# A hybrid mLSTM and stick-breaking layer: gate rows in 128-byte runs, one block transposition, other copy buffers, and a later place for a sigmoid

## The chip, the cores and the metric

The kernel runs on one NeuronCore of one Trainium2 chip. A NeuronCore has five engines that run side by side, each with a queue of its own that is worked off in order: TensorE (PE in the profile, with its weight loads as PEld), VectorE (DVE), ScalarE (ACT), GpSimd (POOL) and SyncE (SP). SyncE computes nothing; here it issues most of the DMAs. An engine that waits for a semaphore holds up everything that stands behind the waiting instruction in its queue. The metric is the device time of one execution in microseconds; lower is better.

## The reference, cut to what matters

One layer on x of shape (1, 512, 1024), float32. A normalised input is projected to all columns at once; two token mixers (an mLSTM with 4 heads of 256, a stick-breaking attention with 8 heads of 128) work on parts of the projection, and their outputs are gated, merged and projected back.

```python
h = rmsnorm(x, norm_w)
proj = jnp.einsum('bsd,de->bse', h, w_in) + b_in
(mq, mk, mv, mi, mf, mo, mz, sq, sk, sv, sz, gates) = jnp.split(proj, split_at, axis=-1)

qk = jax.nn.silu(causal_depthwise_conv(jnp.concatenate([mq, mk], axis=-1), conv_w, conv_b))
mq_c, mk_c = jnp.split(qk, 2, axis=-1)
log_i = mi.astype(jnp.float32).transpose(0, 2, 1)                     # (1, 4, 512)
log_f = jax.nn.log_sigmoid(mf.astype(jnp.float32)).transpose(0, 2, 1) # (1, 4, 512)
hm = mlstm_chunkwise(to_heads(mq_c, M_HEADS), to_heads(mk_c, M_HEADS),
                     to_heads(mv, M_HEADS), log_i, log_f)
hm = rmsnorm(hm..., mlstm_norm_w...)
y_m = hm * jax.nn.sigmoid(mo) * jax.nn.silu(mz)

qs = rmsnorm(to_heads(sq, SB_HEADS), sb_q_norm_w)
ks_ = rmsnorm(to_heads(sk, SB_HEADS), sb_k_norm_w)
y_s = stick_breaking_attention(qs, ks_, to_heads(sv, SB_HEADS)) * jax.nn.silu(sz)

merged = g_m * (y_m @ w_proj_m) + g_s * (y_s @ w_proj_s)   # g = sigmoid(gates)
x = x + merged @ w_out
```

Inside `mlstm_chunkwise` the two gate rows of each head are turned into running sums of log_f and a running maximum; weights are exp(b_t - b_s + i_s - m_t), and the denominator is at least exp(-m_t).

## The kernel before, in words

**Units and steps.** The matrix work is cut into 136 units, listed in `units`. A unit is one block of weights: it is loaded (mostly 128 x 1024 float32 in a `stg` buffer, by SyncE), split into a high and a low part (`split`, L105: ScalarE copies to `wh`, VectorE subtracts to `wl`, L106 and L107), and multiplied in three matmuls per product (`mm3`, L100: high x high, low x high, high x low). For 12 units the low part is made by ScalarE and an accumulating DMA of GpSimd's queue instead (L133 to L135). The main loop (L1492) goes through the units one by one; step c does, in this order: a `slow` callback of unit c-1, the callbacks listed in `later[c]`, the evacuation of unit c-1 out of PSUM (`evac`), the splits of units two steps ahead (`ahead`), the first half of unit c's matmuls (`mm(0)`), the callbacks in `after[c]`, one step of each active generator (the heads), and the second half (`mm(1)`). This order is the order of every engine's queue; nothing is reordered later. A step with 24 matmuls of 512 columns takes about 5.5 us.

**Order of the units.** E is 50. Units 0 to 3 are the attention's first q block, 4 to 7 its first gate, 8 to 49 three `Pair`s, 50 to 65 merge gates and the second attention gate, 66 to 81 the mLSTM's output gates, z gates and the q and k channels of its first two heads, 82 to 97 the same for the other two, then values, gates, both branch projections and the output projection.

**Pairs.** A `Pair` (L965) makes two 512-column blocks with seven products instead of eight, by sums of quarters, in the order 1, 2, 5, 6, 7, 3, 4, each two units long. After products 1, 5 and 6 `copy` (L1015) moves two PSUM banks to SBUF with ScalarE (L1018), as "11", "22" and "12"; after the others `add` (L1021) adds a bank to the bias row with VectorE and lets GpSimd's queue add the copy by an accumulating DMA (`dst<-u`, L1030). Copies 11 and 22 take buffers of the tag `tmp`, of which there are 2; copies 12 take the tag `om`, of which there are 4. Product 7 writes into the bank that copy 12 reads. The q and k norms (`norm`, L396) put the squares that they don't need into an `om` buffer, too (`sqj`).

**Heads.** Each attention head is a generator (`SbSet.head`, L462) that takes one step per unit: splits of q and k, scores, sigmoids into `om` and `a_all` (L489, L493), products along the row by a scan (L501), 32 x 32 transpositions, a round trip through DRAM (`a_d<-ay`, `az<-a_d`), splits into `ath` and `atl` (L553), and the multiplication by the values (`aps<-ath,vh` and so on). The four heads of the second set start at steps 61, 64, 66 and 68. Their values come back from DRAM (`from_dram`, L1049: `vback<-v_park`, issued by SyncE at steps 64, 67, 68 and 69) and are split by ScalarE and VectorE one step later (`v_parts`, L452); no head of that set applies its weights before all four are split.

**Gates.** `gates` (L601, step 49) makes the two gate rows, [4, 512] each, and stores them one step later in DRAM as `i_d` and `f_d`. `gates_scan` (L625, from step 54) is a generator that runs behind the heads in each step. It loads f so that a token is a partition (`by_token`, L621: four DMAs of [128, 4] whose elements lie 2 KB apart in DRAM), makes the log sigmoid on [128, 16] tiles, stores it, loads it back as rows (L656, four DMAs by elements, step 63), does the scans on [4, 512] rows (step 65), stores four results, and loads from them by elements `c_lag[0]` (step 66), `bs` (step 67, the last sum of each block of 128 tokens for all partitions) and `em` (step 68). The `c_lag` tiles are the exponents' offsets per lag between blocks (L680); the mLSTM heads, which start at step 82, use them as a bias (L796) and `em` as the floor of the denominator (L845).

**Convolution.** `MPair.qk_group` (L712) evacuates one block of q or k channels (L716), forms the four taps on VectorE into `acc` (L719, L721), and puts the sigmoid of SiLU (L724, ScalarE, into the same `tmp` buffer) into `after` of the same step, ahead of the heads' step. `prev` does the rest, in three stages at the next q or k unit: the multiplication (L727, VectorE), the high part (L732) and the low part (L736).

The lines of the main loop around the change, shortened:

```python
        units[c].mm(0)
        for fn in after.pop(c, []):
            fn()
        ...
        for g in act:
            if c not in REST and next(g[1], "end") == "end":
                gone.append(g)
        ...
        units[c].mm(1)
```

Of the kernel before, what the change touches and what calls it, by code (L numbers as in the profile page):

```python
# [44 lines left out]
def tile_hybrid_layer(  # L45
# [38 lines left out]
    def blk(tag, dt=F32, shape=(512,), name=None, p=128):  # L84

        where = mp if tag in MISC else sp
        return where.tile([p] + list(shape), dt, name=name or tag, tag=tag, bufs=BUFS[tag])
# [112 lines left out]
        ts = slice(tb * 128, (tb + 1) * 128)  # L200
        return hh[:, k, ts], hl[:, k, ts]

    later, after = {}, {}
    now = [0]

    def defer(n, fn):
# [152 lines left out]
    class SbSet:  # L359
# [36 lines left out]
        def norm(self, name, tb, t):  # L396
            self.raw[name][tb] = t
            ssq = tiny.tile([128, 4], F32, name="ssq", bufs=2)
            rr = tiny.tile([128, 8], F32, name="r" + name, bufs=8 if name == "q" else 4)
            r = rr[:, 0:4]  # L400
            junk = blk("om", BF, (128,), name="sqj")
            for h in range(4):
                nc.scalar.activation(junk, t[:, h * 128:(h + 1) * 128], AF.Square,
                                     accum_out=ssq[:, h:h + 1])
            rstd(r, ssq, 128, EPS)
            self.count[name] += 1
            last = self.count[name] == TB
# [54 lines left out]
        def head(self, h):  # L462
# [101 lines left out]
            def apply(j):  # L564
# [11 lines left out]


    NH = 4
    i_d, f_d, c_d, m_d, b_d, rb_d = [dp.tile([NH, T], F32, name=n)
                                     for n in ("i_d", "f_d", "c_d", "m_d", "b_d", "rb_d")]  # L580
    l_d = dp.tile([128, 16], F32, name="l_d")
    c_lag = [cst.tile([128, TB, NH], F32, name=f"c_lag{k}") for k in range(TB)]
    em = cst.tile([128, TB, NH], F32, name="em")
    gst = cst.tile([128, KT, 8], F32, name="gst")

    wg_t = []
# [14 lines left out]
    def gates():  # L601
        def row(name, p=4):
            return blk("tmp", name=name, p=p)

        wg = wg_t[0]
        ps = att_ps()
        for k in range(KT):
            nc.tensor.matmul(ps, wg[:, k, :], hh[:, k, :], start=k == 0, stop=False)
            nc.tensor.matmul(ps, wg[:, k, :], hl[:, k, :], start=False, stop=k == KT - 1)
        g1 = row("g1", 36)  # L610
        nc.scalar.activation(g1, ps[64:100, :], AF.Copy)
        g2 = row("g2", 36)
        nc.vector.scalar_tensor_tensor(g2, ps[0:36, :], gbias, g1, op0=OP.add, op1=OP.add)

        def store():
            nc.sync.dma_start(i_d, g2[0:4, :])
            nc.sync.dma_start(f_d, g2[32:36, :])

        defer(1, store)

    def by_token(dst, src):  # L621
        for j in range(TB):
            nc.sync.dma_start(dst[:, 4 * j:4 * j + 4], src[:, j * 128:(j + 1) * 128].rearrange("h p -> p h"))

    def gates_scan():  # L625
        def col(name):
            return tiny.tile([128, 16], F32, name=name, bufs=1)


        f, u, w, p = col("gf"), col("gu"), col("gw"), col("gp")  # L630
        by_token(f, f_d)
        yield
        yield
        nc.scalar.activation(u, f, AF.Abs)
# [12 lines left out]
            nc.vector.tensor_scalar(p, p, 2.0 / c, None, op0=OP.add)  # L647
        nc.vector.tensor_tensor(u, u, p, op=OP.mult)
        nc.vector.scalar_tensor_tensor(f, f, 0.0, u, op0=OP.min, op1=OP.subtract)
        nc.sync.dma_start(l_d, f)  # L650
        yield
        yield

        f, gi, m, rb = [blk("y", p=NH, name="g" + name) for name in ("f", "i", "m", "rb")]
        for j in range(TB):
            nc.sync.dma_start(f[:, j * 128:(j + 1) * 128], l_d[:, 4 * j:4 * j + 4].rearrange("p h -> h p"))  # L656
        nc.sync.dma_start(gi, i_d)
        yield
        yield
        nc.vector.tensor_tensor_scan(m, f, gi, 0.0, op0=OP.add, op1=OP.max)  # L660
# [2 lines left out]
            nc.vector.tensor_tensor_scan(b, b, b, 0.0, op0=OP.add, op1=OP.bypass)  # L663
        nc.vector.tensor_tensor(rb, f, m, op=OP.subtract)
        nc.vector.tensor_tensor(gi, gi, f, op=OP.subtract)
        for d, src in ((c_d, gi), (m_d, m), (b_d, f), (rb_d, rb)):
            nc.sync.dma_start(d, src)
        yield
        by_token(c_lag[0].rearrange("p j h -> p (j h)"), c_d)
        yield  # L670
        bs = cst.tile([128, TB, NH], F32, name="bs")
        for j in range(TB):
            nc.sync.dma_start(bs[:, j, :], bass.AP(tensor=b_d.tensor, offset=b_d.offset + 128 * j + 127,
                                                   ap=[[0, 128], [T, NH]]))
        yield
        by_token(em.rearrange("p j h -> p (j h)"), m_d)
        yield
        for k in range(1, TB):
            n = TB - k
            nc.vector.tensor_tensor(c_lag[k][:, 0:n, :], c_lag[k - 1][:, 0:n, :],  # L680
                                    bs[:, k - 1:k - 1 + n, :], op=OP.add)


    P_OFF = [0, 512, 896, 1152]
# [1 line left out]
    class MPair:  # L686
# [25 lines left out]
        def qk_group(self, name, c0, o):  # L712
            def evac(ct, ps):
# [7 lines left out]
                    nc.vector.scalar_tensor_tensor(acc[:, j:], t[:, 0:T - j], cw(3 - j, ch), acc[:, j:],  # L721
                                                   op0=OP.mult, op1=OP.add)
                self.prev()
                after.setdefault(now[0], []).append(lambda: nc.scalar.activation(t, acc, AF.Sigmoid))  # L724

                def mult():
                    nc.vector.scalar_tensor_tensor(t, acc, 1.0 if name == "q" else 0.0625, t,  # L727
# [48 lines left out]
        def head(self, h):  # L776
# [13 lines left out]
            for j in range(TB):  # L790
                lo = j * 128
                w = w_all[:, P_OFF[j]:P_OFF[j] + T - lo]
                for i in range(j, TB):
                    s = slice((i - j) * 128, (i - j + 1) * 128)
                    src = w[:, s] if i == j else rbc[:, i * 128:(i + 1) * 128]
                    nc.scalar.activation(w[:, s], src, AF.Exp, bias=c_lag[i - j][:, j, hd:hd + 1])  # L796
            yield
            while now[0] < M_SCORE[hd] or not ("mk", hd) in done:
                yield
# [31 lines left out]
            def num(i):  # L831
# [10 lines left out]

                st = tiny.tile([128, 4], F32, name="hst", bufs=3)
                dn, ssq, r = st[:, 0:1], st[:, 1:2], st[:, 2:3]
                nc.vector.tensor_scalar(dn, den, -1.0, em[:, i, hd:hd + 1], op0=OP.mult, op1=OP.max)  # L845
                nc.vector.tensor_tensor(dn, dn, den, op=OP.max)
                nc.vector.reciprocal(dn, dn)
                nc.scalar.activation(hn, sum_v, AF.Square, scale=dn, accum_out=ssq)
# [116 lines left out]
    class Pair:  # L965
# [48 lines left out]

        def copy(self, key, q):  # L1015
            for tb in range(2):
                u = blk("om" if q == 12 else "tmp", shape=(516 if q == 12 else 512,), name="u")[:, 0:512]
                nc.scalar.activation(u, self.bank[key, tb], AF.Copy, scale=1.0 if q == 11 else -1.0)  # L1018
                self.dst[q, tb] = u

# [471 lines left out]
    for c in range(N):  # L1492
# [40 lines left out]
        act = [g for g in act if g not in gone] + fresh  # L1533
        act.sort(key=lambda g: g[0])
        fresh, gone = [], []
        units[c].mm(1)
        if c == 1:
            x_turn(3)
    now[0] = N
    units[N - 1].evac()  # L1540
    assert not act and not pend and not later, (act, pend, later)


# [26 lines left out]
```

## Time and profile before

| | |
|---|---|
| median of three runs | 681.55 us (680.84 to 681.89) |
| profiled execution | 682.99 us, of which the span of the program 681.3 us |
| mean granted TensorE clock | 0.997 |
| TensorE matmul busy | 667.6 us, 98% of the span, 3074 instructions |
| VectorE busy | 511.1 us, 75% |
| ScalarE busy | 379.5 us, 56% |
| GpSimd busy | 148.8 us, 22% |

Times in the profile are microseconds from the start of the span. L12 is line 12 of the kernel before. A group of instructions is named by line, engine and "out<-in" with the program's tile names; an engine's name with a q behind it is its sequencer, which issues DMAs and waits. In a timeline a row has start, duration, engine, line, operation, tiles, shapes and count, and in brackets the idle time of the engine just before it and what ended that. In a list of waits the columns are total us, number of times, and the longest. The end of a matmul is modelled: a matmul of 512 columns is shown with 0.39 us, but the next may start 0.23 us after it. A wait for several things is put down to the one that came last.

### The profile page before, as it was taken

How to read it: one execution, taken by the hardware profiler on the slowest of the kernel's cores; microseconds unless marked ns; L12 is line 12 of the kernel's file. 1: busy time of each engine (PE TensorE's matmuls, PEld its weight loads, DVE VectorE, ACT ScalarE, POOL GpSimd, SP SyncE). 2: the span in 40 equal slices, each digit the busy share in tenths (PEclk: the TensorE clock that was granted, in tenths of full speed). 3: DMA queues.
4: the chain of work that ended last, by engine and by line, in shares of the span. 5: the costliest groups of instructions: out<-in, count | busy, mean ns of one | idle time of the engine just before them, and what ended most of it. 6: DMA issues, size and time to landing. Idle time of an engine off the chain costs nothing.

```text
span 681.3 us, 9296 instructions
## 1 busy us (share of the span) xinstructions
PE 667.6 (98%) x3074; PEld 554.4 (81%) x3074; DVE 511.1 (75%) x874; ACT 379.5 (56%) x713; POOL 148.8 (22%) x272
## 2 busy tenths in 40 slices
PE   7999999999999999899899999999999999999997
PEld 5888888887888888688688888888888888888886
DVE  6787988966679798597897845487865656477996
ACT  6576566446776665466443485756456653234451
POOL 4013144214543232154000023222030120001020
PEclk9999999999999999999999999999999999999999
DMA  7567786993869897769862455248631629857332
GB/s 252 142 211 208 218 217 143 330 276 82 193 211 284 265 246 208 178 125 249 202 178 68 137 151 140 62 106 228 207 108 50 214 99 300 292 176 174 105 86 99
DMA packets 131472, 122.99 MB, mean 181 GB/s; under 512 B 17322, under 2 KB 101700, under 8 KB 131424
## 3 DMA queue, kind: packets, MB, share of 16 engines
q1 hardware_dynamic: 122640, 101.82, 50.1%
q0 software_dynamic: 6336, 16.26, 12.9%
q10 hardware_dynamic: 2448, 4.33, 1.7%
q8 instruction: 24, 0.39, 0.2%
q14 instruction: 24, 0.20, 0.1%
HBM read 85.10 MB, written 21.03 MB: 156 GB/s over the span
## 4 chain that ended last, share of the span: by engine, by line
PE 74%; DVE 3%; DMA 3%; issue 1%; ACT 1%; SPq 0%; POOL 0%; DVEq 0%; ACTq 0%; POOLq 0%
PE dps L101 19%; PE dps L103 19%; PE dps L102 19%; PE dps L958 4%; PE aps L102 3%; PE aps L103 3%; PE aps L101 3%; DMA dst<-u 2%; PE aps L958 2%; DMA vback<-v_park 1%; PE aps L838 1%; PE aps L840 1%; PE aps L839 1%; ACT wh L106 1%; DMA tz<-t_d 1%
## 5 line engine op out<-in xcount | busy, mean ns | idle before, releaser
L101 PE MATMUL dps<-hh,wh 128*128 128x512 f32 x448 | 175.6, 392 | 0.1
L103 PE MATMUL dps<-hh,wl 128*128 128x512 f32 x448 | 175.2, 391 | 0.3 <-DMA wl<-stg 0.2
L102 PE MATMUL dps<-hl,wh 128*128 128x512 f32 x448 | 174.9, 391 | 0.0
L107 DVE TENSOR_TENSOR wl<-stg,wh 128x1024 fp32r<-128x1024 f32 x64 | 78.3, 1223 | 59.3 <-ACT wh L106 58.2
L103 PEld LDWEIGHTS dps<-hh,wl 128*128 128x128 f32 x448 | 84.3, 188 | 19.2 <-DMA wl<-stg 1.2
L101 PEld LDWEIGHTS dps<-hh,wh 128*128 128x128 f32 x448 | 84.6, 189 | 16.9 <-issue 0.5
L102 PEld LDWEIGHTS dps<-hl,wh 128*128 128x128 f32 x448 | 84.5, 189 | 16.5
L106 ACT ACTIVATE wh<-stg 128x1024 fp32r<-128x1024 f32 x64 | 67.4, 1055 | 43.1 <-PE dps L102 36.5
L724 ACT ACTIVATE tmp<-acc 128x512 f32<-128x512 f32 x16 | 10.1, 634 | 51.2 <-DVE acc L721 51.2
L721 DVE SCALAR_TENSOR_TENSOR acc<-tmp,vec,acc 128x511 f32<-128x511 f32 (+2 forms) x48 | 36.2, 753 | 1.7
L135 POOL DMA_DIRECT2D wl<-stg x12 | 10.9, 906 | 106.3 <-ACT wl L134 50.6
L491 POOL TENSOR_SCALAR_AFFINE_SELECT om<-om 128x128 f32<-128x128 f32 x32 | 20.4, 638 | 60.9 <-ACT om L489 60.8
L958 PE MATMUL dps<-wh,form 128*128 128x512 f32 x96 | 30.7, 392 | 1.5 <-ACT u L1018 1.5
L958 PE MATMUL aps<-wh,form 128*128 128x512 f32 x96 | 30.5, 389 | 0.0
L107 DVE TENSOR_TENSOR wl<-X,wh 128x1024 fp32r<-128x1024 f32 x18 | 21.9, 1219 | 7.6 <-ACT wh L106 7.6
L106 ACT ACTIVATE wh<-X 128x1024 fp32r<-128x1024 f32 x18 | 19.0, 1058 | 15.1 <-PE aps L958 11.1
L1030 POOL DMA_DIRECT2D dst<-u x18 | 16.0, 1030 | 51.2 <-DVE dst L1027 34.2
L501 DVE TENSOR_TENSOR_SCAN om<-om 128x512 f32<-128x512 f32 (+3 forms) x32 | 26.3, 823 | 0.0
L101 PE MATMUL dps<-yh,wh 128*128 128x512 f32 x64 | 24.9, 389 | 0.0
L102 PE MATMUL dps<-yl,wh 128*128 128x512 f32 x64 | 24.9, 389 | 0.0
L103 PE MATMUL dps<-yh,wl 128*128 128x512 f32 x64 | 24.9, 389 | 0.0
L958 PEld LDWEIGHTS dps<-wh,form 128*128 128x128 f32 x96 | 18.0, 188 | 6.1 <-ACT u L1018 2.3
(292 smaller groups left out, 1595.6 us busy)
## 6 DMA issues: line engine op xcount, KB each, us to landing
stg<-in_w_in_dram SPq DMA_DIRECT2D x63, 512.0 KB, 4.7
wl<-stg POOLq DMA_DIRECT2D x12, 512.0 KB, 5.5
a_d<-ay SPq DMA_DIRECT2D x8, 640.0 KB, 6.2
az<-a_d SPq DMA_DIRECT2D x32, 160.0 KB, 4.5
dst<-u POOLq DMA_DIRECT2D x18, 256.0 KB, 5.4
t_d<-ty SPq DMA_DIRECT2D x8, 512.0 KB, 3.5
tz<-t_d SPq DMA_DIRECT2D x32, 128.0 KB, 5.0
stg<-in_w_proj_s_dram SPq DMA_DIRECT2D x8, 512.0 KB, 4.1
```

The costliest lines, as they stand in the source:

```text
L101: nc.tensor.matmul(ps, ah, bh, start=first, stop=False)
L102: nc.tensor.matmul(ps, ah, bl, start=False, stop=False)
L103: nc.tensor.matmul(ps, al, bh, start=False, stop=last)
L106: nc.scalar.activation(hi, src, AF.Copy)
L107: nc.vector.tensor_tensor(lo, src, hi.bitcast(F32), op=OP.subtract)
L135: nc.gpsimd.dma_start(out=self.wl, in_=self.st, accum_op=OP.add)
L491: nc.gpsimd.affine_select(out=om[:, ts], in_=om[:, ts], compare_op=OP.is_gt, fill=1.0, base=0, channel_multiplier=1, pattern=[[-1, 128]])
L501: nc.vector.tensor_tensor_scan(back, back, back, 1.0, op0=OP.mult, op1=OP.bypass)
L721: nc.vector.scalar_tensor_tensor(acc[:, j:], t[:, 0:T - j], cw(3 - j, ch), acc[:, j:], op0=OP.mult, op1=OP.add)
L724: after.setdefault(now[0], []).append(lambda: nc.scalar.activation(t, acc, AF.Sigmoid))
L958: nc.tensor.matmul(pr.bank[key, tb], a, w[:, i, :], start=begin and n == 0, stop=end and n == 2, skip_group_check=again)
L1030: nc.gpsimd.dma_start(out=t, in_=u[tb], accum_op=OP.add)
```

## The change

Five edits:

- The gate rows f and i lie in one DRAM tensor `fi_d` of [2, 4, 512], so do c and m in `cm_d`. A tensor of 4,096 elements is loaded in one DMA as 128 runs of 32 elements (128 bytes): partition 32a + n gets tokens 32a to 32a + 31 of block n, where n counts (tensor, head, block of 128 tokens). The log sigmoid is taken elementwise in this layout, for i as well, whose result isn't used, and stored with the same pattern; the scan's rows are then plain rows of DRAM. For c and m the [128, 32] tile is turned by one VectorE transposition of 32 x 32 blocks, after which a token is a partition again, with c in columns 0 to 15 and m in 16 to 31.
- Of b only the last element of each block is stored (16 elements, `bl_d`), and `bs` is one broadcast load of 64 bytes per partition. The `c_lag` and `em` tiles have the head ahead of the block.
- The scan's loads come in one step (67), and the tiles are made in step 70, where it was 69.
- `Pair.copy` puts "22" in `om` instead of `tmp`, and the squares of `norm` go to a tile of their own.
- The sigmoid of the convolution goes into a new list `last`, which runs after the heads' step and ahead of `mm(1)`, for steps before 80 (the evacuations at steps 71, 73, 75, 77 and 79, five of 16).

```diff
-    later, after = {}, {}
+    later, after, last = {}, {}, {}
...
-            junk = blk("om", BF, (128,), name="sqj")
+            junk = tiny.tile([128, 128], BF, name="sqj", bufs=1)
...
-    i_d, f_d, c_d, m_d, b_d, rb_d = [dp.tile([NH, T], F32, name=n)
-                                     for n in ("i_d", "f_d", "c_d", "m_d", "b_d", "rb_d")]
-    l_d = dp.tile([128, 16], F32, name="l_d")
-    c_lag = [cst.tile([128, TB, NH], F32, name=f"c_lag{k}") for k in range(TB)]
-    em = cst.tile([128, TB, NH], F32, name="em")
+    fi_d, l_d, cm_d = [dp.tile([2, NH, T], F32, name=n) for n in ("fi_d", "l_d", "cm_d")]
+    rb_d = dp.tile([NH, T], F32, name="rb_d")
+    bl_d = dp.tile([NH, TB], F32, name="bl_d")
+    cm = cst.tile([128, 32], F32, name="cm")
+    c_lag = [cm[:, 0:16].rearrange("p (h j) -> p h j", h=NH)]
+    c_lag += [cst.tile([128, NH, TB], F32, name=f"c_lag{k}") for k in range(1, TB)]
+    em = cm[:, 16:32].rearrange("p (h j) -> p h j", h=NH)
...
-    def by_token(dst, src):
-        for j in range(TB):
-            nc.sync.dma_start(dst[:, 4 * j:4 * j + 4], src[:, j * 128:(j + 1) * 128].rearrange("h p -> p h"))
+    def runs(t):
+        return bass.AP(tensor=t.tensor, offset=t.offset, ap=[[32, 4], [128, 32], [1, 32]])
...
-        by_token(f, f_d)
+        nc.sync.dma_start(f, runs(fi_d))
...
-        nc.sync.dma_start(l_d, f)
+        nc.sync.dma_start(runs(l_d), f)
...
-        for j in range(TB):
-            nc.sync.dma_start(f[:, j * 128:(j + 1) * 128], l_d[:, 4 * j:4 * j + 4].rearrange("p h -> h p"))
-        nc.sync.dma_start(gi, i_d)
+        nc.sync.dma_start(f, l_d[0])
+        nc.sync.dma_start(gi, fi_d[1])
...
-        for d, src in ((c_d, gi), (m_d, m), (b_d, f), (rb_d, rb)):
+        for d, src in ((cm_d[0], gi), (cm_d[1], m), (bl_d, f[:, 127::128]), (rb_d, rb)):
             nc.sync.dma_start(d, src)
         yield
-        by_token(c_lag[0].rearrange("p j h -> p (j h)"), c_d)
         yield
-        bs = cst.tile([128, TB, NH], F32, name="bs")
-        for j in range(TB):
-            nc.sync.dma_start(bs[:, j, :], bass.AP(tensor=b_d.tensor, offset=b_d.offset + 128 * j + 127,
-                                                   ap=[[0, 128], [T, NH]]))
+        bs = cst.tile([128, NH, TB], F32, name="bs")
+        nc.sync.dma_start(u, runs(cm_d))
+        nc.sync.dma_start(bs.rearrange("p h j -> p (h j)"),
+                          bass.AP(tensor=bl_d.tensor, offset=bl_d.offset, ap=[[0, 128], [1, NH * TB]]))
         yield
-        by_token(em.rearrange("p j h -> p (j h)"), m_d)
         yield
+        yield
+        nc.vector.transpose(cm, u)
...
-                after.setdefault(now[0], []).append(lambda: nc.scalar.activation(t, acc, AF.Sigmoid))
+                (last if now[0] < E + 30 else after).setdefault(now[0], []).append(lambda: nc.scalar.activation(t, acc, AF.Sigmoid))
...
-                u = blk("om" if q == 12 else "tmp", shape=(516 if q == 12 else 512,), name="u")[:, 0:512]
+                u = blk("tmp" if q == 11 else "om", shape=(512 if q == 11 else 516,), name="u")[:, 0:512]
...
+        for fn in last.pop(c, []):
+            fn()
         units[c].mm(1)
```

More of the change, by code (lines that the diff above doesn't have):

```diff
@@ L615, in store @@
         def store():
-            nc.sync.dma_start(i_d, g2[0:4, :])
-            nc.sync.dma_start(f_d, g2[32:36, :])
+            nc.sync.dma_start(fi_d[1], g2[0:4, :])
+            nc.sync.dma_start(fi_d[0], g2[32:36, :])
         defer(1, store)
-    def by_token(dst, src):
-        for j in range(TB):
-            nc.sync.dma_start(dst[:, 4 * j:4 * j + 4], src[:, j * 128:(j + 1) * 128].rearrange("h p -> p h"))
+    def runs(t):
+        return bass.AP(tensor=t.tensor, offset=t.offset, ap=[[32, 4], [128, 32], [1, 32]])
     def gates_scan():
         def col(name):
-            return tiny.tile([128, 16], F32, name=name, bufs=1)
+            return tiny.tile([128, 32], F32, name=name, bufs=1)
         f, u, w, p = col("gf"), col("gu"), col("gw"), col("gp")
-        by_token(f, f_d)
+        nc.sync.dma_start(f, runs(fi_d))
         yield
@@ L665, in gates_scan @@
         nc.vector.tensor_tensor(gi, gi, f, op=OP.subtract)
-        for d, src in ((c_d, gi), (m_d, m), (b_d, f), (rb_d, rb)):
+        for d, src in ((cm_d[0], gi), (cm_d[1], m), (bl_d, f[:, 127::128]), (rb_d, rb)):
             nc.sync.dma_start(d, src)
         yield
-        by_token(c_lag[0].rearrange("p j h -> p (j h)"), c_d)
         yield
-        bs = cst.tile([128, TB, NH], F32, name="bs")
-        for j in range(TB):
-            nc.sync.dma_start(bs[:, j, :], bass.AP(tensor=b_d.tensor, offset=b_d.offset + 128 * j + 127,
-                                                   ap=[[0, 128], [T, NH]]))
+        bs = cst.tile([128, NH, TB], F32, name="bs")
+        nc.sync.dma_start(u, runs(cm_d))
+        nc.sync.dma_start(bs.rearrange("p h j -> p (h j)"),
+                          bass.AP(tensor=bl_d.tensor, offset=bl_d.offset, ap=[[0, 128], [1, NH * TB]]))
         yield
-        by_token(em.rearrange("p j h -> p (j h)"), m_d)
         yield
+        yield
+        nc.vector.transpose(cm, u)
         for k in range(1, TB):
             n = TB - k
-            nc.vector.tensor_tensor(c_lag[k][:, 0:n, :], c_lag[k - 1][:, 0:n, :],
-                                    bs[:, k - 1:k - 1 + n, :], op=OP.add)
+            nc.vector.tensor_tensor(c_lag[k][:, :, 0:n], c_lag[k - 1][:, :, 0:n],
+                                    bs[:, :, k - 1:k - 1 + n], op=OP.add)
     P_OFF = [0, 512, 896, 1152]
@@ L795, in head @@
                     src = w[:, s] if i == j else rbc[:, i * 128:(i + 1) * 128]
-                    nc.scalar.activation(w[:, s], src, AF.Exp, bias=c_lag[i - j][:, j, hd:hd + 1])
+                    nc.scalar.activation(w[:, s], src, AF.Exp, bias=c_lag[i - j][:, hd, j:j + 1])
             yield
@@ L844, in num @@
                 dn, ssq, r = st[:, 0:1], st[:, 1:2], st[:, 2:3]
-                nc.vector.tensor_scalar(dn, den, -1.0, em[:, i, hd:hd + 1], op0=OP.mult, op1=OP.max)
+                nc.vector.tensor_scalar(dn, den, -1.0, em[:, hd, i:i + 1], op0=OP.mult, op1=OP.max)
                 nc.vector.tensor_tensor(dn, dn, den, op=OP.max)
@@ L1540, in tile_hybrid_layer @@
     units[N - 1].evac()
-    assert not act and not pend and not later, (act, pend, later)
+    assert not act and not pend and not later and not last, (act, pend, later)
 _INS = ["x", "norm_w", "w_in", "b_in", "conv_w", "conv_b", "mlstm_norm_w",
```

## The prediction

> **What bounds the kernel now.** I read the page first, then the waits of TensorE (columns: total us, times, longest), then the windows around those waits. From the page:
>
> ```profile
> PE 667.6 (98%) x3074; PEld 554.4 (81%) x3074; DVE 511.1 (75%) x874; ACT 379.5 (56%) x713; POOL 148.8 (22%) x272
> DMA packets 131472, 122.99 MB, mean 181 GB/s; under 512 B 17322, under 2 KB 101700, under 8 KB 131424
> ```
>
> and from the waits of TensorE, all that lie behind the first 15 us:
>
> ```profile
> PE aps L102 <- DVE atl L107: 2.2, 3, 1.8
> PE aps L101 <- ACT ath L106: 2.0, 2, 1.0
> PE dps L958 <- ACT u L1018: 1.5, 2, 1.3
> PE dps L103 <- DMA wl<-stg: 0.2, 1, 0.2
> ```
>
> TensorE sets the time: behind its first microseconds it stops for nothing but these eight waits, so an edit is worth what it takes from them and nothing more. A wait costs more than its figure, since that counts from the modelled end of the matmul before. So I looked at windows (PE, PEld, DVE, ACT, POOL busy with counts; then granted clock, DMA share, GB/s):
>
> ```profile
> 283.00:288.00 5.00, 2.28 (x10) 1.37 (x9) 4.52 (x7) 4.60 (x10) 1.75 (x5) 1.00 1.15 305
> 288.00:292.00 4.00, 4.00 (x13) 3.44 (x12) 3.93 (x8) 4.00 (x8) 2.17 (x3) 0.57 0.30 119
> 313.00:348.00 35.00, 33.09 (x148) 25.91 (x146) 29.03 (x57) 18.20 (x29) 5.22 (x11) 1.00 0.88 224
> 265.00:348.00 83.00, 78.37 (x354) 63.57 (x353) 67.89 (x132) 45.10 (x77) 23.68 (x45) 0.98 0.83 204
> 348.00:662.00 314.00, 313.87 (x1474) 263.31 (x1473) 217.78 (x352) 164.23 (x280) 43.14 (x86) 1.00 0.52 149
> ```
>
> After 348 us nothing is left to win until the tail, which the change doesn't touch. Before it, there are three places: two short waits in the pairs (A), one long stall at 284 us (B), a cluster at 313 to 348 us (C). Each edit has one of them to itself or shares it.
>
> **A, the copies.** TensorE (timeline: start, duration, what) and what held ScalarE:
>
> ```profile
> 117.29 0.50 PE L958 MATMUL dps<-wh,form 128*128 128x512 f32 x1 [0.20 <-ACT u L1018]
> ...
> 155.28 0.39 PE L958 MATMUL dps<-wh,form 128*128 128x512 f32 x1
> 156.94 0.50 PE L958 MATMUL dps<-wh,form 128*128 128x512 f32 x1 [1.27 <-ACT u L1018]
> ```
>
> ```profile
> ACT u L1018 <- DMA dst<-u: 9.1, 5, 3.2
> ```
>
> The product-5 copy ("22", L1018) takes a `tmp` buffer, of which there are two, both still held by product 1's copies until their accumulating DMA has read them. ScalarE stands there, and behind it stand two weight splits and product 6's copy, for which product 7's first matmul waits. In `om` there are four buffers, 22 and 12 use two each, and the squares that used to take `om` in between go to a tile of their own. So the wait goes. What is late next is the copy itself, which starts when the bank is done, as in the first pair, where TensorE doesn't wait. Matmuls of this shape start 0.23 us apart (next fence, 283.38 to 283.60). Lost: 156.94 - 155.28 - 0.23 = 1.43, which is the idle 1.27 and 0.16 that the modelled end hides (0.39 - 0.23); by the same rule 0.20 + 0.16 = 0.36 at 117.29. Together **1.8 us**. If a head's `om` had to wait for the last pair's DMA instead, that falls in a step with no TensorE wait now; I take 0 for it and put up to 0.5 us into the range.
>
> **B, the gate loads ahead of the value load.** TensorE:
>
> ```profile
> 283.38 0.39 PE L102 MATMUL dps<-hl,wh 128*128 128x512 f32 x1
> 283.60 0.39 PE L103 MATMUL dps<-hh,wl 128*128 128x512 f32 x1
> 284.96 0.50 PE L101 MATMUL aps<-ath,vh 128*128 128x512 f32 x1 [0.97 <-ACT ath L106]
> 287.22 0.50 PE L102 MATMUL aps<-atl,vh 128*128 128x512 f32 x1 [1.75 <-DVE atl L107]
> 287.56 0.40 PE L103 MATMUL aps<-ath,vl 128*128 128x512 f32 x1
> ...
> 291.78 0.39 PE L101 MATMUL dps<-hh,wh 128*128 128x512 f32 x1
> ```
>
> SyncE's queue:
>
> ```profile
> 272.10 4.36 SPq L656 DMA_DIRECT2D gf<-l_d  x4
> 276.57 1.74 SPq L657 DMA_DIRECT2D gi<-i_d  x1
> 278.35 0.35 SPq L1051 DMA_DIRECT2D vback<-v_park  x1
> 278.74 1.85 SPq L443 DMA_DIRECT2D tz<-t_d  x4
> ```
>
> ScalarE:
>
> ```profile
> 282.81 0.63 ACT L455 ACTIVATE vh<-vback 128x512 fp32r<-128x512 f32 x1 [8.36 <-DMA vback<-v_park]
> ```
>
> From 272.10 to 278.31 SyncE pushes four element gathers and the blocked load behind them; only then goes `vback`, landing 4.46 us later (282.81 - 278.35). ScalarE is idle for it, and the split that TensorE needs stands behind it. After the change there are two plain row loads. Each issue costs between 0.35 (the `vback` row) and 1.74 us (the `gi` row); I take 0.46, a quarter of the `tz` row's 1.85, which is nearest to a queue that isn't blocked. `vback` then goes at about 273.0 and lands by 277.5, 5.3 us sooner; TensorE, which started 2.15 us after vh did (284.96 - 282.81), could start at about 279.7 and asks at 283.83. Even at 1.74 each it is 2.7 us sooner and the first wait is gone. VectorE's half goes with it: its row ends 287.17 at present, 5.3 us sooner is 281.9, before 284.06.
>
> Lost there: 284.96 - 283.60 - 0.23 = 1.13; 287.22 - 284.96 - 0.23 = 2.03; 0.34 instead of 0.23 for the next, 0.11; then the 4.22 us from 287.56 to 291.78 hold seven 512-wide and six 384-wide matmuls (one and three left of the two applied blocks, three of a score, six of the projection), 7 x 0.23 + 6 x 0.17 (three quarters) = 2.63 at their normal pitch: 1.59 us lost, at a granted clock of 0.57. Sum **4.8 us** and a little; by the worse issue price about 4.
>
> The half clock follows 2.72 us of idle time in two pieces. The Trainium skill (TensorE: Matmul & The Clock Gate, Part 1) has the array re-throttled after an idle window of about 3.4 us; by that the 1.59 us would not be due to this stall and would stay, which makes 3.3 instead of 4.8 here. The trace's order, stall and then half clock, speaks for 4.8.
>
> **C, the later gate loads and the conv sigmoid.** SyncE, ScalarE and TensorE:
>
> ```profile
> 306.18 6.32 SPq L623 DMA_DIRECT2D em<-m_d  x4
> 312.61 2.60 SPq L1051 DMA_DIRECT2D vback<-v_park  x1
> ```
>
> ```profile
> 317.58 0.63 ACT L455 ACTIVATE vh<-vback 128x512 fp32r<-128x512 f32 x1 [3.16 <-DMA vback<-v_park]
> ...
> 329.94 0.63 ACT L724 ACTIVATE tmp<-acc 128x512 f32<-128x512 f32 x1 [5.71 <-DVE acc L721]
> 330.48 1.03 ACT L106 ACTIVATE ath<-az 128x384 fp32r<-128x384 f32 x2
> ```
>
> ```profile
> 329.62 0.39 PE L103 MATMUL dps<-hh,wl 128*128 128x512 f32 x1
> 331.04 0.38 PE L101 MATMUL aps<-ath,vh 128*128 128x256 f32 x1 [1.03 <-ACT ath L106]
> 331.63 0.39 PE L102 MATMUL aps<-atl,vh 128*128 128x256 f32 x1 [0.21 <-DVE atl L107]
> ```
>
> Lost: 331.04 - 329.62 - 0.23 = 1.19, and 331.63 - 331.04 - 0.12 (half the columns) = 0.47. The window 313 to 348 has 35.00 - 33.09 = 1.91 us idle, 1.24 of it in these two; the other 0.67 lies in some four short waits, each hiding 0.16 more, and each of the six is followed by a matmul 0.11 us late, as at 287.56: 0.67 + 0.16 x 4 + 0.11 x 6 = 1.97. C is 1.19 + 0.47 + 1.97, about **3.6 us** in all.
>
> Two edits meet here. The `em` gathers (6.32 us of SyncE, then 2.60 us to issue `vback`) are gone from this place; `vback` lands up to 8 us sooner, and ScalarE's 3.16 us before 317.58 with it. Weight halves that are loaded by accumulating DMA (`wl<-stg`) no longer share the rings with elements. And the sigmoid that held ScalarE for 5.71 us now stands behind the heads' splits, so ath at 330.48 could run from about 324. Either alone removes the 1.19; they don't add. VectorE's atl comes behind the convolution in its own queue in any case. I take 2.9 of the 3.6 and leave 0.7 for that.
>
> Costed at nothing: gate columns of 32 instead of 16, one transposition, one step more until the c_lag tiles are made. They run in steps where TensorE has no wait in the list above, and the first reader of c_lag comes at step 83, thirteen steps on. If that cover were gone, their own busy time would be the price, under 1 us as estimated from the tile sizes beside ScalarE's 0.63 us for 512 columns. The moved sigmoid is read by VectorE at its next visit:
>
> ```profile
> 339.77 0.68 DVE L727 SCALAR_TENSOR_TENSOR tmp<-acc,tmp 128x512 f32<-128x512 f32 x1
> ```
>
> That is 9.2 us after the sigmoid ended at 330.57, and the heads' work that now comes first is a few instructions of 0.4 to 0.7 us: nothing.
>
> **Sum.** 1.8 + 4.8 + 2.9 = 9.5 us. The profiled execution took 682.99 us with a span of 681.3; it becomes 673.5 with a span of 671.8. Its 682.99 is 1.4 above the median of 681.55, from which the same sum gives **672.0**. All of A, B and C is 10.2.
>
> **Rivals.**
> *VectorE becomes the bound.* It is busy 67.89 of 83.00 us from 265 to 348; less B and C, 8.4 us, that is 91%. Where its queue is late, the waits for atl stay: B's second (2.03) and nearly all of C. For it: three of the eight waits are for VectorE. Against it: it stands idle ahead of 283.5 in the very gap that B closes, so its work moves forward too. Gain 1.8 + 2.8 + 0.5 = 5.1: 676.4. Chance 0.13.
> *The new loads hold the queue as the old ones did.* From the page:
>
> ```profile
> em<-m_d SPq DMA_DIRECT2D x4, 2.0 KB, 9.2
> ```
>
> If one 128-packet load took these 9.2 us and blocked SyncE, `vback` would stay late, and only A and the sigmoid's 1.2 would be won: 678.6. Against it: five groups of 2,048 elements become 128 runs each, and of 17,322 small packets some 10,000 go. This also is the case in which the change doesn't do what it says. Chance 0.08. The Trainium skill (DMA: Bandwidth & Descriptors, Why a DMA increments its semaphore by 16 and not by 1) has the number of engines chosen by the slowest dimension; the new pattern's is 4, so by it four engines carry 32 packets each, an estimate as many per engine as one old gather of 512 on sixteen. By that rule a load isn't quicker than one of the old, but there is one for four, and the sum stays.
> *The stalls move* to another wait of the same size: 681.5, chance 0.03.
> *Slower.* The five moved sigmoids stand behind the heads' splits; if one waits there for a late `az` load, VectorE stops at L727 and with it the weight halves of the next step. It decides once the sigmoid is over 9.2 us late at the first site; four such sites at 3 us each, less A, would be 681.55 + 12 - 1.8 - 4.8 = 687. Against it: the loads get earlier. Chance 0.03.
>
> **How the numbers follow.** The forecast holds 0.73. Low end: all 10.2 gives 671.3; the median of three moves by some 0.5 (they ran from 680.84 to 681.89), 670.8, and 0.1 for the estimated small waits, 670.7. High end: VectorE's case at 676.4 and a little, 676.8. These leave out the last three rivals and some of the edges. A measurement of this kernel tells 0.2% (1.4 us) from no change: faster 0.94, same 0.03, slower 0.03.
>
> **What would show it.** SyncE's row for `gf<-l_d` is a single issue under 1 us and `vback` goes by 274; ScalarE's wait for `vback` at 283 shrinks under 1 us; no window at 0.57 clock behind it. The waits of TensorE for u (L1018) are gone from the list. ath no longer follows L724. Packets under 512 B fall to about 8,000. Wrong would be: a wait for atl of over 1 us (VectorE), a 4 us SyncE issue (rings), idle time ahead of L727 (sigmoid).

## The result and the profile after

The changed kernel takes **673.04 us** (median of four, 672.67 to 674.32); the kernel before takes 681.72 us on the same chip. The ratio is 0.9878, with a 95% interval of 0.9861 to 0.9895: 8.3 us faster, 7.2 to 9.5. The profiled execution took 673.08 us, which is 9.91 less than the one before, with a span of 671.4.

From the page of the changed kernel (busy time of each engine; DMA packets by size):

```profile
PE 664.3 (99%) x3074; PEld 553.9 (83%) x3074; DVE 511.7 (76%) x875; ACT 381.2 (57%) x713; POOL 144.3 (21%) x272
DMA packets 121376, 123.00 MB, mean 183 GB/s; under 512 B 7226, under 2 KB 91604, under 8 KB 121328
```

and all its waits of TensorE (total us, times, longest):

```profile
PE dps L1407 <- DVE idle L1402: 1.5, 1, 1.5
PE dps L1439 <- DVE hh L318: 1.3, 1, 1.3
PE aps L102 <- DVE atl L107: 0.2, 1, 0.2
PE aps L314 <- DVE x L306: 0.2, 1, 0.2
```

Three of the four lie in the first 15 us, which the change doesn't touch. Of the eight waits behind them one is left, 0.2 us long. The work of TensorE is the same, 3,074 matmuls; small packets fell by 10,096. The windows of the changed kernel, columns as in the prediction:

```profile
275.00:290.00 15.00, 15.00 (x75) 12.76 (x74) 14.65 (x26) 8.75 (x16) 6.47 (x12) 1.00 0.65 187
265.00:348.00 83.00, 82.65 (x390) 69.02 (x390) 74.72 (x143) 49.87 (x83) 18.27 (x41) 1.00 0.77 210
```

From 265 to 348 us TensorE was idle for 4.63 us and is now idle for 0.35; in the same 83 us it starts 390 matmuls instead of 354. No half clock is left, and VectorE is busier (74.72 instead of 67.89) because it, too, stopped standing still. SyncE's queue in the changed kernel:

```profile
269.45 0.26 SPq L655 DMA_DIRECT2D gf<-l_d  x1
269.81 0.25 SPq L656 DMA_DIRECT2D gi<-fi_d  x1
270.11 0.35 SPq L1050 DMA_DIRECT2D vback<-v_park  x1
...
303.47 0.32 SPq L1050 DMA_DIRECT2D vback<-v_park  x1
```

The two gate loads take 0.51 us to issue, where the five took 6.1; `vback` follows at 270.11 instead of 278.35, and ScalarE waits 0.56 us for it instead of 8.36:

```profile
272.73 0.63 ACT L455 ACTIVATE vh<-vback 128x512 fp32r<-128x512 f32 x1 [0.56 <-DMA vback<-v_park]
```

What is left of the cluster (TensorE; two blocks of heads):

```profile
323.23 0.37 PE L101 MATMUL aps<-ath,vh 128*128 128x384 f32 x1
323.75 0.45 PE L102 MATMUL aps<-atl,vh 128*128 128x384 f32 x1
...
329.65 0.28 PE L101 MATMUL aps<-ath,vh 128*128 128x256 f32 x1
330.14 0.39 PE L102 MATMUL aps<-atl,vh 128*128 128x256 f32 x1 [0.21 <-DVE atl L107]
```

The pairs start 0.52 and 0.49 us apart, where 0.18 and 0.12 is usual: 0.34 and 0.37 us for VectorE's atl, in every kernel below.

To compare all kernels by place, I took from each trace the time from one matmul's start to the next one's, less the usual pitch of its shape (0.227 us for 512 columns), wherever it was more than 0.06 us over; this is called "lost" below. A is the two waits for u, B the stall at about 284 us with the half clock behind it, C the cluster up to 348 us. For the kernel before it gives A 2.0, B 4.85, C 3.8 us; for the changed one 0, 0 and 1.0. The difference is 9.6 us of the 9.91 between the two profiles.

### The profile page after: what moved, and what is told of

The parts are those of the page before. It is cut to its first block, busy times and chain, and to the rows that moved or that the text cites. A ratio compares the mean times of both kernels' runs of the same rounds, so it can differ in the third digit from the quotient of the medians.

```text
span 671.4 us, 9281 instructions
## 1 busy us (share of the span) xinstructions
PE 664.3 (99%) x3074; PEld 553.9 (83%) x3074; DVE 511.7 (76%) x875; ACT 381.2 (57%) x713; POOL 144.3 (21%) x272
## 2 busy tenths in 40 slices
DMA packets 121376, 123.00 MB, mean 183 GB/s; under 512 B 7226, under 2 KB 91604, under 8 KB 121328
## 4 chain that ended last, share of the span: by engine, by line
PE 96%; DVE 2%; DMA 1%; issue 0%; SPq 0%; ACT 0%; DVEq 0%
PE dps L101 22%; PE dps L103 21%; PE dps L102 21%; PE dps L957 10%; PE aps L957 7%; PE aps L102 3%; PE aps L103 3%; PE aps L101 3%; PE dps L1439 1%; PE dps L1441 1%; PE dps L1440 1%; PE aps L837 1%; PE aps L839 1%; PE aps L838 1%; DMA stg<-in_w_in_dram 1%; PE aps L314 0%
## 5 line engine op out<-in xcount | busy, mean ns | idle before, releaser
L489 ACT ACTIVATE om<-aps,rq 128x512 f32<-128x512 f32 (+3 forms) x32 | 16.7, 523 | 9.2 <-PE aps L103 8.9
```

What stands on the lines that cost most here:

```text
L489: nc.scalar.activation(om[:, 0:n], zp, AF.Sigmoid, scale=rn[:, h:h + 1])
```

## Experiments: each edit alone

**The gate edit alone.** The kernel before with all of the gate part of the diff, but not the copies and not the sigmoids.

```diff
+    fi_d, l_d, cm_d = [dp.tile([2, NH, T], F32, name=n) for n in ("fi_d", "l_d", "cm_d")]
...
-        by_token(f, f_d)
+        nc.sync.dma_start(f, runs(fi_d))
...
+        nc.vector.transpose(cm, u)
```

> Only the gate edit (runs of 128 bytes, bl_d, the transposition); copies and sigmoid as before. My theory, three separate places: B (4.8 us) and nearly all of C (2.9 us, since the earlier values and the moved sigmoid cure the same wait) go, A (1.8 us) stays: about 674.5 us against 681.7, and the waits of TensorE list L1018 with 1.5 us again. Rival 1, the sigmoid edit is needed for C as well: 1.2 us less gain, 675.7, with a wait for ath of about 1 us behind L724. Rival 2, removing A's wait is what let B's loads go early: gain under 4 us.

Measured: 676.40 us beside 682.58, ratio 0.9903 (0.9884 to 0.9922): 6.6 us less, 5.3 to 7.9. Its waits of TensorE from 100 to 350 us:

```profile
PE dps L957 <- ACT u L1017: 1.1, 2, 0.9
PE aps L102 <- DVE atl L107: 0.4, 2, 0.2
```

B is gone, C is down to 1.4 us lost, and A is as it was (1.7). The gate edit is what most of the gain comes from.

**The copies alone.**

```diff
-            junk = blk("om", BF, (128,), name="sqj")
+            junk = tiny.tile([128, 128], BF, name="sqj", bufs=1)
...
-                u = blk("om" if q == 12 else "tmp", ...
+                u = blk("tmp" if q == 11 else "om", ...
```

> Only copy 22 in om and the squares in a tile of their own. My theory: the two waits for u (1.8 us) go, B and C stay as they were: about 679.9 us against 681.7; TensorE has no wait for L1018, and the window behind the stall at about 286 us still has half the clock. Rival, the time is given back at B, because the loads that land late there don't move with TensorE: 681.7, no difference.

Measured: 680.29 beside 682.58, ratio 0.9966 (0.9954 to 0.9977): 2.3 us less, 1.6 to 3.1. Its waits in the same stretch:

```profile
PE aps L102 <- DVE atl L107: 2.2, 3, 1.8
PE aps L101 <- ACT ath L106: 1.4, 2, 0.9
PE dps L103 <- DMA wl<-stg: 0.6, 1, 0.6
```

The wait for u is off the list, B and C stay. Gates and copies add: 6.6 + 2.3 = 8.9.

**The sigmoids alone, and the changed kernel without them.**

```diff
-                after.setdefault(now[0], []).append(lambda: nc.scalar.activation(t, acc, AF.Sigmoid))
+                (last if now[0] < E + 30 else after).setdefault(now[0], []).append(...)
...
+        for fn in last.pop(c, []):
+            fn()
```

> Only the five sigmoids behind the heads' step. My theory: the wait for ath near 330 us goes from 1.0 to 0.2 or less, the one for atl behind it stays near 0.4 because VectorE does the taps first: gain 0.8 to 1.2 us, 680.7 against 681.7. Rival, the sigmoid now stands behind a split that waits for a buffer, and VectorE's multiplication (L727) waits for it: no gain or a loss of up to 2 us, with idle time ahead of L727.

> The changed kernel with the sigmoids put back ahead of the heads' step. My theory: with the gate loads gone the sigmoid no longer matters: 673.0 to 673.5 us, the ratio to the changed kernel under 1.001; ScalarE has slack in front of ath. Rival: the sigmoid's 1.2 us come on top, 674.2 us, and a wait for ath of about 1 us stands in the list again.

Measured: alone 681.35 beside 682.58, ratio 0.9975 (0.9961 to 0.9990), 1.7 us less (0.7 to 2.7). The changed kernel without them: 673.91 beside 682.58, ratio 0.9866 (0.9847 to 0.9885), 9.1 us less, no different from the whole change. Waits of the kernel with the sigmoids alone:

```profile
PE aps L102 <- DVE atl L107: 1.9, 2, 1.8
PE dps L958 <- ACT u L1018: 1.7, 2, 1.5
PE aps L101 <- ACT ath L106: 0.5, 1, 0.5
PE dps L103 <- DMA wl<-stg: 0.4, 1, 0.4
```

The 0.5 for ath is that of B; the one of C has gone. In that kernel C loses 1.9 us instead of 3.8. In the changed kernel it loses 1.0 with the sigmoid edit and 1.4 without, which the times can't tell apart. So the sigmoid edit cures something the gate edit also cures.

## Experiments: what makes B and C

**The first loads alone.** Only the loads of f, i and l as runs (steps 54 to 64); c, m and the block sums still go by elements, so the `em` gathers stay.

```diff
-        by_token(f, f_d)
+        nc.sync.dma_start(f, runs(fi_d))
...
-        for j in range(TB):
-            nc.sync.dma_start(f[:, j * 128:(j + 1) * 128], l_d[:, 4 * j:4 * j + 4].rearrange("p h -> h p"))
-        nc.sync.dma_start(gi, i_d)
+        nc.sync.dma_start(f, l_d[0])
+        nc.sync.dma_start(gi, fi_d[1])
```

> The kernel before with only the first half of the gate edit: f, i and the log sigmoid in runs of 128 bytes, so that the two loads of step 63 are plain rows; c, m and b stay gathers by elements, copies and sigmoid stay. My theory: B is the work of the queue at step 63 alone, so B goes (4.8 us) and C stays: 676.9 us against 681.7. Rival: the elements of the later gathers, which share rings with the loads, are a part of B too: gain under 3 us, a wait for ath near 284 us stays.

Measured: 675.16 beside 683.25, ratio 0.9881 (0.9857 to 0.9905), 8.1 us less, 6.5 to 9.8. SyncE's queue and the waits of TensorE from 100 to 350 us:

```profile
299.06 5.39 SPq L622 DMA_DIRECT2D em<-m_d  x4
305.28 0.33 SPq L1052 DMA_DIRECT2D vback<-v_park  x1
```

```profile
PE dps L959 <- ACT u L1019: 1.6, 2, 1.3
PE aps L102 <- DVE atl L107: 0.3, 2, 0.2
```

The `em` gathers still hold the queue for 5.39 us, and yet, against what I expected, C is down to 1.1 us lost, all at atl. The first loads alone gain as much as the whole gate edit did (6.6 us, 5.3 to 7.9): the runs of the second loads and the transposition add nothing to it that these runs can tell.

**The second loads alone.** The reverse: c, m and the block sums in runs, f, i and l by elements.

```diff
+        nc.sync.dma_start(u, runs(cm_d))
...
-        by_token(em.rearrange("p j h -> p (j h)"), m_d)
...
+        nc.vector.transpose(cm, u)
```

> The kernel before with only the second half of the gate edit: c and m in one load of runs and a transposition, the last sums of b packed; f and the log sigmoid stay gathers by elements. My theory: B stays, with half the clock behind it, and C loses the waits for wl and for ath: gain 1.5 to 2.9 us, 679.3 against 681.7. Rival: C is late because TensorE's stall at B has shifted the engines against each other, then C goes with the first half instead and nothing is gained here.

Measured: 682.05 beside 683.25, ratio 0.9982 (0.9968 to 0.9995), 1.2 us less, 0.3 to 2.2, where I expected 1.5 to 2.9. Of SyncE, ScalarE and TensorE (waits):

```profile
311.85 0.32 SPq L1058 DMA_DIRECT2D vback<-v_park  x1
```

```profile
315.75 0.63 ACT L455 ACTIVATE vh<-vback 128x512 fp32r<-128x512 f32 x1 [2.36 <-DMA vback<-v_park]
317.23 1.05 ACT L134 ACTIVATE wl<-stg 128x1024 fp32r<-128x1024 f32 x1
```

```profile
PE aps L102 <- DVE atl L107: 2.3, 4, 1.8
PE dps L965 <- ACT u L1025: 1.6, 2, 1.4
PE dps L103 <- DMA wl<-stg: 1.4, 1, 1.4
PE aps L101 <- ACT ath L106: 1.0, 2, 0.8
```

No gathers stand ahead of the last `vback`, and it goes at 311.85, hardly before the 312.61 of the kernel before. ScalarE waits for it still (2.36 us; 3.16 before), the copy into wl behind it is late, and TensorE waits for that weight half: C loses 3.8 us as before. What holds SyncE here is the buffer: set 1's `vback` takes `brow`, of which there is one, and may be loaded only when VectorE's vl (L456) has read the one before. SyncE's waits for that line, 285 to 316 us:

```profile
SPq L1058 <- DVE vl L456: 5.8, 2, 3.7
```

**The order on the queue.** The kernel before, all loads by elements, with one more `yield` after the store of l, so that the five gate loads, and all that the scan does after them, come one step later: the five loads behind the `vback` of step 64.

```diff
         nc.sync.dma_start(l_d, f)
         yield
         yield
+        yield
```

> The kernel before, all gathers by elements kept, but everything of the gate scan from the second load on one step later. So the value load of step 64 goes ahead of the gathers on SyncE's queue, and the one of step 69 ahead of em's; that of step 68 comes behind c_lag's, that of 69 behind bs's. My theory: the order on SyncE's queue is what counts, not the elements on the rings: B goes for the most part (3 to 4.8 us), the last value load is 6 us sooner, and the gain is 4 to 6 us, 676.5 us. Rival: the elements slow the transfers themselves; the value load still lands after 282 us, the gain is under 1.5 us.

Measured: 678.91 beside 683.25, ratio 0.9940 (0.9920 to 0.9959), 4.1 us less, 2.8 to 5.5. SyncE:

```profile
272.33 0.34 SPq L1052 DMA_DIRECT2D vback<-v_park  x1
...
275.16 7.70 SPq L657 DMA_DIRECT2D gf<-l_d  x4
...
303.37 5.23 SPq L674 DMA_DIRECT2D bs<-b_d  x4
308.71 2.17 SPq L1052 DMA_DIRECT2D vback<-v_park  x1
```

The gathers are as slow as ever, and B is gone: what counts for B is who stands in front of `vback`. C came out worse (4.8 us lost; ath waits 1.7), I think because the gathers of the block sums now fall ahead of the last `vback`.

**A second buffer for vback.** Three kernels have this edit: the second loads alone, the kernel before, and the changed kernel.

```diff
-        t = blk("om", shape=(516,), name="vback")[:, 0:512] if n else blk("brow", name="vback")
+        t = blk("om", shape=(516,), name="vback")[:, 0:512] if n else blk(("brow", "acc")[tb % 2], name="vback")
```

> The kernel of the second loads alone (c, m and the block sums in runs, the first loads still by elements), with one more edit: the set-1 value loads (vback, n = 0) alternate between the buffers brow and acc, so that a load need not wait for VectorE's vl of the one before. With the second loads alone the last vback was issued at 311.85 us, behind vl, wl<-stg was waited for 1.57 us at 325, and the kernel took 682.05 us beside 683.25 of the kernel before. Theory 1, the single buffer makes the stretch of 313 to 348 us late: the last vback goes by 306, the waits for wl<-stg (1.57) and ath (0.42) at 325 to 330 go, the stall at 284 us stays; 2.0 to 2.5 us less than the second loads alone, about 679.7 beside 683.2. Theory 2, VectorE's own queue is late by the stall at 284 us, and the buffer only shows it: vback goes sooner, but vl runs when it ran (316.97, counted from the stall), the waits stay, and the time stays within 0.7 us of 682.

> The kernel before with one edit: set-1 vback alternates between brow and acc. The em gathers (6.32 us of SyncE) stay ahead of the last vback. Theory 1 (single buffer decides, the gathers alone don't): the last vback no longer waits for vl at 311.3, but still for the gathers; it goes between 306 and 312.6, and the time falls by 0.3 to 1.5 us. Theory 2 (VectorE's queue is late anyway): within 0.5 us of the kernel before, waits for wl<-stg and ath as before. The prediction's reading (em gathers make it late, whatever the buffer): the last vback stays near 312 and the time within 0.5 us; the split from theory 2 is in the issue time of vback.

> The changed kernel with the one edit: set-1 vback alternates between brow and acc. What is left for it are the waits for atl of 0.34 and 0.37 us at 323 to 330 us, which theory 1 and theory 2 both put down to VectorE's own work: 672.4 to 673.3 us beside 673.0 of the changed kernel, so no difference that these rounds can tell; faster than 672.4 would say that the buffer still costs something.

Measured, beside 682.36 of the kernel before: second loads 680.73, ratio 0.9978 (0.9966 to 0.9990); before 681.02, ratio 0.9981 (0.9971 to 0.9990); changed 673.37, ratio 0.9870 (0.9855 to 0.9885). SyncE in the first of them, and then in the second:

```profile
304.01 0.32 SPq L1058 DMA_DIRECT2D vback<-v_park  x1
```

```profile
303.62 6.73 SPq L623 DMA_DIRECT2D em<-m_d  x4
310.44 2.64 SPq L1051 DMA_DIRECT2D vback<-v_park  x1
```

Together with the two kernels above that makes a square. With gathers and one buffer the last `vback` goes at 312.61, with gathers and two at 310.44, with runs and one at 311.85, with runs and two at 304.01. Each of the two holds it alone; only without both is it early. In that last kernel the wait for wl is gone and C loses 1.5 us in the profiled execution, as theory 1 had it; but against the second loads alone (0.9982) the time hardly moved, and the last vl ran 33.5 us after the vl of the stall, as it did with one buffer (33.2), which is what theory 2 said. That execution also had the half clock behind B, which puts TensorE later by itself, while the one with a single buffer had not. So what the buffer is worth isn't settled by these runs. In the kernel before it gave 1.3 us (0.7 to 2.0), near the top of what theory 1 allowed, with C as large as ever (4.1 us lost) and the wait for wl still there; the wait isn't where it came from, and the cause stays open. In the changed kernel it gives nothing, and the changed kernel stays the best.

## Experiment: half clock behind a stall

The changed kernel with unused work added at step 117: a transposition on TensorE, six dependent copies of its result on ScalarE, and a transposition of that, so that TensorE stands still once, far from everything else.

```diff
+        ps, t = att_ps(), tiny.tile([128, 128], F32, name="stall", bufs=1)
+        nc.tensor.transpose(ps[:, 0:128], ident, ident)
+        nc.scalar.activation(t, ps[:, 0:128], AF.Copy)
+        for _ in range(5):
+            nc.scalar.activation(t, t, AF.Copy)
+        nc.tensor.transpose(ps[:, 128:256], t, ident)
...
+    after.setdefault(n_gates + 11, []).append(stall)
```

> The changed kernel with one stall put in at step 117, where TensorE runs without waits: it makes a transposition, ScalarE copies the result six times over, and TensorE turns the last copy. Nothing of this is used. I expect a wait of 2.4 to 3.1 us. My theory, that a stall of that length has the clock halved behind it as at B: matmuls 0.43 us apart for about 3.3 us, 1.6 us more than the stall itself. Rival, by the page on TensorE of the Trainium skill (Part 1, idle window of about 3.4 us): no half clock, the matmuls start 0.23 us apart at once.

> The kernel of the artificial stall (5 unused ScalarE copies between two matmuls at step 117) once more, timed in three rounds, to see whether the half clock behind a stall of some 2.2 us comes each time. If the idle time alone decides it, every execution is 4.5 to 5.3 us above the changed kernel (673.0), some 677.5 to 678.4, with a mean granted clock of 0.997. If it comes only in some, there are executions at a mean clock of 1.0 some 1.6 us below the others, 676 to 677. A stall that never leads to it again would put the single look down to chance.

Measured: one execution of 678.37 us first, and seven of 675.6 to 680.66 (median 677.86) later. The wait is 2.07 us, where I expected 2.4 to 3.1. TensorE in the first, with the window behind the stall:

```profile
604.75 0.27 PE L1478 MATMUL aps<-ident 128*128 128x128 f32 x1
607.09 0.33 PE L1482 MATMUL aps<-ident,stall 128*128 128x128 f32 x1 [2.07 <-ACT stall L1481]
```

```profile
607.00:611.00 4.00, 3.91 (x11) 3.09 (x12) 0.91 (x1) 0.04 (x1) 0.00 (x0) 0.57 0.60 117
```

and in the profiled one of the seven:

```profile
606.83 0.27 PE L1478 MATMUL aps<-ident 128*128 128x128 f32 x1
609.18 0.33 PE L1482 MATMUL aps<-ident,stall 128*128 128x128 f32 x1 [2.07 <-ACT stall L1481]
```

```profile
609.20:613.00 3.80, 3.80 (x18) 3.16 (x19) 1.48 (x2) 0.95 (x1) 0.00 (x0) 1.00 0.50 113
```

The same stall, to a hundredth of a microsecond (2.34 and 2.35 us from start to start; 2.24 beyond the usual 0.11 of this shape): behind the one come 11 matmuls in 4 us at a clock of 0.57, behind the other 18 in 3.8 us at 1.00. The half clock costs 1.6 us (seven matmuls at a pitch of 0.43 us instead of 0.23, and two in between), and a stall of this length may or may not bring it. Of the seven executions the two with a mean clock of 0.999 or more took 675.6 and 676.12 us, the five at 0.997 or less 677.41 to 680.66; the trace of one of those five shows a half clock at 11 to 14 us, behind a wait of 2.8 us in the kernel's start, so the mean alone doesn't say where it fell.

## Why the prediction was right, and where it wasn't

**A, 1.8 us: right.** The trace of before loses 2.0 there (the late second matmul, 0.11 each time, was left out of this term), and the copies alone gave 2.3 (1.6 to 3.1). ScalarE has no wait for the accumulating DMA at u left; its waits at that line are for TensorE's bank, but for one of 1.9 us for a store (`z_park<-tmp`). It now waits for that DMA at one of the squares (`sqj<-dst`, 4.49 us at 168.72), where TensorE doesn't wait behind it.

**B, 4.8 us: the mechanism right, the size that of one execution.** The single issues (0.26 and 0.25 us, below the 0.35 that was given as the lower bound), `vback` at 270.11, no half clock: each stands in the rows above, and the kernel with the gathers merely behind `vback` shows that the order in SyncE's queue was the cause. But the stall itself varies. Over the six profiles that have it, it cost 4.85, 4.46, 4.29, 3.05, 4.27 and 2.65 us (before, copies alone, sigmoids alone, second loads alone, and the second-buffer kernels of second loads and before). The two smallest have no half clock:

```profile
288.00:292.00 4.00, 4.00 (x21) 3.44 (x20) 3.93 (x9) 3.70 (x8) 2.17 (x4) 1.00 0.38 148
```

is the window behind the stall in the second loads alone, beside the 0.57 of the kernel before. Here the step failed that took the whole sum from the median: "from which the same sum gives 672.0". The profiled execution had the largest B of the six; with their mean, 3.9, the sum is 8.6 and the forecast 672.9 (681.55 - 8.6), beside 673.04 measured. Against its own execution the sum was close: 673.5 forecast, 673.08 found. That the spread of B is the whole of the missing microsecond fits, but five of the six kernels have an edit elsewhere. Whether the half clock costs the whole kernel its 1.59 us the executions of the kernel before leave open: beside the three groups of experiments, the 18 with a mean granted clock of 0.999 or more have medians 0.2, 1.6 and 0.3 us below those of the 45 with less, wherever in the kernel the lower clock fell.

The Trainium skill (TensorE: Matmul & The Clock Gate, Part 1) has the cold state come after at least one idle window of about 3.4 us. The traces show it behind one stall of 2.24 us and not behind another of the same length, so a shorter idle time can be enough; the prediction was right not to go by 3.4, and wrong to count the 1.59 us as certain.

**C, 2.9 us of 3.6: the size right (3.8 to 1.0) by luck, the cause wrong in its first link.** The failed step is "The `em` gathers (6.32 us of SyncE, then 2.60 us to issue `vback`) are gone from this place; `vback` lands up to 8 us sooner". Without the gathers, but with B and the single buffer, the last `vback` went at 311.85 instead of 312.61 and C stayed at 3.8; with the gathers, but without B, it went at 305.28 and C fell to 1.1. Whether the weight halves land sooner for want of elements, as the prediction had it, the rows leave open: the accumulating DMA (`wl<-stg`) issued at 305.11 in the kernel before took 9.2 us to land, the same one 9.0 in the changed kernel and 5.6 in the second loads alone.

What does hold over all the profiles is the part of the step behind `vback`. With the sigmoids in their old place, ScalarE waits 2.36 to 3.55 us for the last `vback` in five kernels, and C is 3.6 to 4.8 there; in the six kernels where it doesn't wait, with the sigmoids in either place, C is 1.0 to 1.5. The sigmoids alone lie between (2.65 and 1.9). The second loads with two buffers are among the six (C 1.5), B and its half clock included; but the times didn't follow there, and it is one execution of each kernel. So `vback` was late for two reasons, either of them enough: the gathers, and the single buffer, which ties it to a VectorE that B had made late.

By way of that buffer C was, I think, in the main a consequence of B. VectorE's rows say how, first and last vl of set 1 in the kernel before:

```profile
283.48 0.69 DVE L456 TENSOR_TENSOR vl<-vback,vh 128x512 fp32r<-128x512 f32 x1 [7.00 <-ACT vh L455]
...
318.24 0.69 DVE L456 TENSOR_TENSOR vl<-vback,vh 128x512 fp32r<-128x512 f32 x1 [1.14 <-ACT vh L455]
```

and in the changed one:

```profile
274.17 0.65 DVE L456 TENSOR_TENSOR vl<-vback,vh 128x512 fp32r<-128x512 f32 x1
...
308.61 0.65 DVE L456 TENSOR_TENSOR vl<-vback,vh 128x512 fp32r<-128x512 f32 x1
```

From the first to the last it takes 34.8 us in the one and 34.4 in the other, with waits of 1.8 and 1.9 us in between: VectorE works through nearly the same queue in the same time, and the last `vback`, in its single buffer, is tied to it. But it starts 9.3 us sooner. In B VectorE stood still for 7.00 us and TensorE lost 4.85. When B went, VectorE (with 2.0 from A) came 9.3 us forward and TensorE 6.9, and those 2.4 us of lead are more than any wait of C (1.19 at most). This is worked out from rows; no kernel tested the lead by itself. The kernel of the order fits it: there VectorE came 6.9 us forward at first and 4.2 at the last vl (276.59 and 314.02), lost its lead, and C stayed.

"Either alone removes the 1.19; they don't add" held: the sigmoids alone took that wait away, and beside the gate edit they are worth nothing that can be measured.

**Costed at nothing: right.** The transposition, on VectorE,

```profile
315.50 0.17 DVE L676 STREAM_TRANSPOSE cm<-gu 128x32 f32<-128x32 f32 x1
```

falls where TensorE waits for nothing. On ScalarE the moved sigmoid ran right behind the heads' split:

```profile
322.58 0.52 ACT L106 ACTIVATE ath<-az 128x384 fp32r<-128x384 f32 x1 [5.55 <-PE aps L102]
323.01 0.61 ACT L723 ACTIVATE tmp<-acc 128x512 f32<-128x512 f32 x1
```

and VectorE read its product at 330.00, 6.4 us after its end. ScalarE's 5.55 us are now a wait for TensorE.

**The rivals.** VectorE as the bound: no wait for atl over 1 us, so no, though it is what the last 1.0 us of C waits for. New loads that hold the queue: issues of 0.25 to 1.08 us (the longest `gf<-fi_d` at 199.67, far from any wait), and 7,226 small packets beside the 8,000 forecast; how many engines carried such a load no row here shows. Stalls that move and late sigmoids: neither was seen.

## What to carry to other kernels

Price a stall by what it does to every engine's queue, not only to the one that sets the time: an engine that loses more than TensorE does can be late once more 40 us on. Here curing the first stall took most of the second with it, without touching what stood there; in the kernel of the order, where other loads then stood in the way, it didn't. Where two things hold the same transfer (a queue and a buffer), removing one shows little. And a term that comes out of one profiled execution, above all a half clock, shouldn't be taken whole from a median.

## What the runs showed of the hardware

- The half clock is no function of the stall's length alone: 2.24 us from start to start, beyond the usual, brought 3.4 us of it once and none another time, in the same program at the same place. At B 2.57 us lost in two pieces brought it (second loads with two buffers) and 2.94 didn't (second loads alone). The waits for u of 1.1 to 1.6 us never did in the profiles here.
- Four gathers of 512 single elements hold SyncE's queue for 2 to 8 us, and not by a fixed price: `gf<-l_d` took 4.36 us in the kernel before and 7.70 us one step later, among other traffic. One load in runs of 128 B, of as many bytes as eight such gathers, took 0.68 us to issue (`gu<-cm_d` in the changed kernel), another 1.08 (`gf<-fi_d`).
